# Layer norm from pairwise sums on VectorE and ScalarE, right Strassen factors in a two-engine pipeline, and deferred lower halves in one stage only

## The chip, the core and the metric

The kernel runs on one core of one Trainium2 chip. The metric is the time of one execution in device microseconds (us). TensorE (PE) multiplies, VectorE (DVE) and ScalarE (ACT) do the elementwise work and empty PSUM, GpSimd (POOL) does elementwise work from SBUF to SBUF and issues some DMAs, and SyncE (SP) issues most DMAs. Each engine executes its own instructions in the order in which the program wrote them, and waits for another engine where an operand or a buffer asks for it.

## What is computed

One inference step of a decoder of four layers, 512 prompt positions and 8 sample positions (520 columns in all), model width 1024. Each layer has a token mixer (sparse attention, gated MLP, gated recurrence, sparse attention) and a feed-forward part, and each of the two is followed by a residual sum and a layer norm:

```python
def layer_norm(x, g, b):
    mu = jnp.mean(x, axis=-1, keepdims=True)
    var = jnp.mean(jnp.square(x - mu), axis=-1, keepdims=True)
    return (x - mu) * lax.rsqrt(var + LN_EPS) * g + b

def swiglu_ffn(x, w_in, w_out):
    gate, up = jnp.split(x @ w_in, 2, axis=-1)
    return (jax.nn.silu(gate) * up) @ w_out

for layer in range(4):
    x = layer_norm(ALPHA * x + mixer(x), ...)
    x = layer_norm(ALPHA * x + swiglu_ffn(x, ...), ...)
```

The gated MLP of layer 1 has one more layer norm, on its `v`. So there are nine norms over 520 columns.

## The kernel before

Data lies transposed: the 1024 features are eight blocks of 128 partitions, the 520 columns lie along the free axis, and are worked on in two halves, columns 0 to 255 (the first half) and 256 to 519 (the second half).

**Split products.** Every matrix product runs as three fp32r products: each weight and each activation is split into an upper half (a cast on ACT, L145 for weights, L291 for activations) and a lower half (the source minus the upper half, on DVE, L147 and L292), and `mm` (L330 to L332) multiplies upper by upper, lower by upper and upper by lower. `Weights.need` runs the list of weight splits 5 steps ahead of the one that is used; a step is 4 blocks of k, that is 12 matmuls. `Weights.split` writes the cast at once, but with `lag` on it keeps the lower half back until the next split is written (`flush`). `lag` is on during the whole feed-forward part.

**Ticks.** `mm` calls `tick` after every second k, that is after 6 matmuls. A tick advances every spawned generator by its rate. Layer norm, the right factors and `bounds` are such generators, so their instructions are written between the matmuls of whatever comes next.

**Layer norm** (`ln`, L345). The last product of a half writes the sums over the eight blocks (L442, L444: POOL, the last one DVE). After `WM` = 3 ticks a matmul with a matrix of 1/1024 (L359) gives the mean. Then for four pairs of blocks DVE subtracts it (L366) and ACT squares (L367); DVE reduces each four squared blocks to one row by a strided reduction (L375, two of them); two matmuls (L380) add the two rows over the partitions; ACT and DVE form the reciprocal root (L421 to L434); DVE multiplies by it (L388); ACT writes the upper half with gain and bias (L393); POOL writes the normalised x in place with gain and bias (L397); DVE forms the lower half from x and the upper half (L353), so it waits for POOL. In the last norm's second half `direct` leaves the reductions out and multiplies all eight squared blocks by the matrix.

The out projection goes through the first half of all blocks before the second half, and the next phase begins with first halves only. So the norm of the first half runs beside the out projection's second half, and the norm of the second half beside the first six weight units of the next phase: six times 8 k-blocks of 3 matmuls, 24 ticks.

**Feed-forward.** The 22 hidden blocks are worked on in chunks of 8, 7 and 7. The first 3 blocks of chunk 0 are plain products, whose first halves come first; the others are pairs by Strassen's scheme in Winograd's form, 7 products each (`gated`), in an order that `products` makes. The right factors T1 to T4 are differences of blocks of x, made once (`right`), spawned at the first second-half product at one step per tick: DVE (T3: POOL, L507) writes a difference into an `fsum` tile, ACT casts it, DVE subtracts, and then comes the next. The products of a pair add up in three PSUM banks, by `bank = "xyxzyxx"[q]`; ACT copies bank x out after products 0, 2 and 5 (L577). In the last pair products 5 and 6 are neighbours, both in bank x.

`bounds` prepares constants of layer 2 during the feed-forward part of layer 1, from its 40th tick on: an activation table, one exponential, and some DVE instructions of 32 elements.

## Time and profile before

| what | value |
| --- | --- |
| median of 3 runs | 2996.29 us (2993.99 to 2998.5) |
| the profiled execution | 2996.22 us |
| its span, first to last instruction | 2994.5 us |
| PE busy | 2777.2 us, 93% |
| DVE busy | 2005.7 us, 67% |
| ACT busy | 1555.9 us, 52% |
| POOL busy | 835.3 us, 28% |
| chain of waits that ended last | PE 68%, DVE 16%, ACT 8% |
| granted PE clock, mean | 0.977 |

The profiled execution lies at the median of the runs, and 1.7 us lie outside its span. The engines' shares are averages over stages with different limits. The question for every stage is what PE waits for there.

### The profile page before, as it was taken

How to read it: one execution, taken by the hardware profiler on the slowest of the kernel's cores; microseconds unless marked ns; L12 is line 12 of the kernel's file. 1: busy time of each engine (PE TensorE's matmuls, PEld its weight loads, DVE VectorE, ACT ScalarE, POOL GpSimd, SP SyncE). 2: the span in 40 equal slices, each digit the busy share in tenths (PEclk: the TensorE clock that was granted, in tenths of full speed). 3: DMA queues.
4: the chain of work that ended last, by engine and by line, in shares of the span. 5: the costliest groups of instructions: out<-in, count | busy, mean ns of one | idle time of the engine just before them, and what ended most of it. 6: DMA issues, size and time to landing. Idle time of an engine off the chain costs nothing.

```text
span 2994.5 us, 56333 instructions
## 1 busy us (share of the span) xinstructions
PE 2777.2 (93%) x21818; PEld 2647.2 (88%) x21818; DVE 2005.7 (67%) x4221; ACT 1555.9 (52%) x3474; POOL 835.3 (28%) x787
## 2 busy tenths in 40 slices
PE   7999888999989899998999989999899998899997
PEld 7888568999989899998999989999898875799997
DVE  4788656565756765677677677566768877574665
ACT  4666535454545453554455545345456665453553
POOL 0222134332330432333100033233312222342342
PEclk9999999999999999999999999999999999999998
DMA  4222533555423245562222235556222244345551
GB/s 177 65 64 70 178 127 95 139 156 145 140 78 97 56 130 138 138 173 86 69 83 84 70 104 136 139 140 171 84 89 64 64 135 144 110 120 137 149 158 45
DMA packets 167678, 340.39 MB, mean 114 GB/s; under 512 B 15474, under 2 KB 78450, under 8 KB 167410
## 3 DMA queue, kind: packets, MB, share of 16 engines
q1 hardware_dynamic: 147840, 281.79, 29.6%
q0 software_dynamic: 12096, 44.05, 8.5%
q10 hardware_dynamic: 7474, 10.95, 1.0%
q8 instruction: 172, 2.82, 0.4%
q14 instruction: 96, 0.79, 0.1%
HBM read 323.46 MB, written 13.27 MB: 112 GB/s over the span
## 4 chain that ended last, share of the span: by engine, by line
PE 68%; DVE 16%; ACT 8%; issue 3%; POOL 2%; DMA 2%; SPq 0%; ACTq 0%; POOLq 0%; DVEq 0%
PE ps L330 10%; PE ps L332 10%; PE ps L331 10%; PE ps L530 9%; PE ps L531 8%; PE ps L532 8%; POOL x L397 2%; DVE row L375 2%; ACT g L1164 1%; PE ps L1034 1%; DVE g L1162 1%; PE ps L1211 1%; PE ps L855 1%; PE ps L1160 1%; PE ps L1195 1%
## 5 line engine op out<-in xcount | busy, mean ns | idle before, releaser
L330 PE MATMUL ps<-g 128*128 128x256 f32 (+1 forms) x3744 | 1096.5, 293 | 21.5 <-ACT g L145 13.9
L331 PE MATMUL ps<-g 128*128 128x256 f32 (+1 forms) x3744 | 1070.3, 286 | 29.9 <-DVE g L147 27.2
L332 PE MATMUL ps<-g 128*128 128x256 f32 (+1 forms) x3744 | 1071.2, 286 | 3.4 <-DVE g L292 1.8
L331 PEld LDWEIGHTS ps<-g 128*128 128x128 f32 x3744 | 720.0, 192 | 38.2 <-DVE g L147 29.6
L330 PEld LDWEIGHTS ps<-g 128*128 128x128 f32 x3744 | 720.7, 192 | 34.9 <-ACT g L145 14.1
L332 PEld LDWEIGHTS ps<-g 128*128 128x128 f32 x3744 | 717.8, 192 | 4.6 <-DVE g L292 2.6
L147 DVE TENSOR_TENSOR g<-g 128x512 fp32r<-128x512 f32 x708 | 580.0, 838 | 126.0 <-ACT g L145 125.2
L530 PE MATMUL ps<-g 128*128 128x260 f32 x2128 | 603.6, 284 | 17.5 <-ACT frow L577 17.5
L531 PE MATMUL ps<-g 128*128 128x260 f32 x2128 | 602.1, 283 | 0.0
L532 PE MATMUL ps<-g 128*128 128x260 f32 x2128 | 601.9, 283 | 0.0
L145 ACT CAST g<-g 128x512 fp32r<-128x512 f32 (+1 forms) x788 | 462.0, 607 | 144.8 <-PE ps L332 78.6
L530 PEld LDWEIGHTS ps<-g 128*128 128x128 f32 x2128 | 401.9, 189 | 20.8 <-ACT frow L577 20.8
L532 PEld LDWEIGHTS ps<-g 128*128 128x128 f32 x2128 | 402.1, 189 | 0.0
L531 PEld LDWEIGHTS ps<-g 128*128 128x128 f32 x2128 | 402.1, 189 | 0.0
L577 ACT ACTIVATE frow<-ps 128x260 f32<-128x260 f32 x304 | 117.9, 388 | 247.3 <-PE ps L532 247.3
L1164 ACT ACTIVATE g<-g,nst 128x128 f32<-128x128 f32 (+3 forms) x256 | 143.1, 559 | 123.0 <-DVE nst L1162 120.8
L147 DVE TENSOR_TENSOR g<-fsum,g 128x512 fp32r<-128x512 f32 x228 | 165.1, 724 | 38.3 <-ACT g L145 38.3
L147 POOL TENSOR_TENSOR g<-g 128x512 fp32r<-128x512 f32 x80 | 105.6, 1326 | 249.6 <-ACT g L145 239.1
L1176 POOL TENSOR_SCALAR g<-g,nst 128x128 f32<-128x128 f32 (+3 forms) x64 | 75.9, 1186 | 345.2 <-DVE nst L1169 237.5
L586 POOL TENSOR_TENSOR frow<-frow 128x260 f32<-128x260 f32 x64 | 47.8, 747 | 428.7 <-ACT frow L577 428.7
L180 POOL TENSOR_TENSOR fsum<-g 128x512 f32<-128x512 f32 x76 | 120.9, 1591 | 130.8 <-DMA g<-ffn_in 110.8
L145 ACT CAST g<-fsum 128x512 fp32r<-128x512 f32 x228 | 133.9, 616 | 41.3 <-PE ps L332 41.3
(270 smaller groups left out, 4047.7 us busy)
## 6 DMA issues: line engine op xcount, KB each, us to landing
g<-ffn_in SPq DMA_DIRECT2D x176, 512.0 KB, 4.5
g<-ffn_in POOLq DMA_DIRECT2D x76, 512.0 KB, 5.9
g<-ffn_out SPq DMA_DIRECT2D x64, 448.0 KB, 3.7
g<-nsa_in SPq DMA_DIRECT2D x42, 512.0 KB, 4.3
fsum<-ffn_in SPq DMA_DIRECT2D x76, 256.0 KB, 3.6
cm<-cache_cmp SPq DMA_DIRECT2D x64, 256.0 KB, 3.9
g<-cache_slc SPq DMA_DIRECT2D x128, 128.0 KB, 2.8
g<-cache_win SPq DMA_DIRECT2D x32, 512.0 KB, 4.4
```

What stands on the lines that cost most here:

```text
L145: self.nc.scalar.copy(h, src)
L147: self.subs.append(lambda: (eng or self.nc.vector).tensor_sub(l, src, h.bitcast(FT)))
L180: nc.gpsimd.tensor_add(t[x], t[p], t[q])
L330: nc.tensor.matmul(p[:, :n], H[:, s], a, start=k == 0, stop=False)
L331: nc.tensor.matmul(p[:, :n], L[:, s], a, start=False, stop=False)
L332: nc.tensor.matmul(p[:, :n], H[:, s], b, start=False, stop=k == nk - 1)
L530: nc.tensor.matmul(p, H[:, s], a, start=start and k == 0, stop=False, skip_group_check=True)
L531: nc.tensor.matmul(p, L[:, s], a, start=False, stop=False, skip_group_check=True)
L532: nc.tensor.matmul(p, H[:, s], b, start=False, stop=k == 3, skip_group_check=True)
L577: nc.scalar.activation(s[q], p, AF.Copy, scale=-1.0 if q in (1, 5) else 1.0)
L1164: defer(lambda P=P, i=i: (self.table(LN_EXP), nc.scalar.activation(P, P, AF.Exp, bias=st[:, i:i + 1], scale=-1.0, accum_out=st[:, 4 + i:5 ...
L1176: eng.tensor_scalar(P, P, st[:, 4 + i:5 + i], None, op0=OP.mult)
```

## The change

In `ln`, the reduction is replaced by three additions of 512 or 528 elements, and the matmuls take the two blocks that are left (`direct` is gone, the last norm goes the same way). The squares are written in one tick. `WV` = 2 more ticks lie ahead of the variance matmul. The multiplication by the reciprocal root also applies the gain, one block at a time (two instructions for a pair instead of one). ACT adds the bias when it writes the upper half, DVE forms the lower half from x, the bias and the upper half, and ACT adds the bias to x in place one tick later. POOL is left with one addition for each pair in the norms that write no halves (the gated MLP's and the last).

```diff
-            if j % 2:
-                yield
-        for j in range(2):
-            if direct:
-                q += [sq[j][:, i] for i in range(4)]
-            else:
-                q.append(self.row()[:, :n])
-                nc.vector.tensor_reduce(q[-1], sq[j].rearrange("p b t -> p t b"), op=OP.add, axis=AX.X)
-            yield
+            if j == 3:
+                yield
+        for s in sq:
+            nc.vector.tensor_add(s[:, :2], s[:, :2], s[:, 2:])
+        yield
+        nc.vector.tensor_add(sq[0][:, :2], sq[0][:, :2], sq[1][:, :2])
...
-            nc.vector.tensor_mul(xs, xs, y[:, None, :].to_broadcast([128, 2, n]))
...
+                nc.vector.scalar_tensor_tensor(xs[:, k], xs[:, k], self.gn[:, li, 2 * j + k:2 * j + k + 1], y,
+                                               op0=OP.mult, op1=OP.mult)
             if X is not None:
...
+                for k in (0, 1):
+                    nc.scalar.activation(h[:, k], xs[:, k], AF.Identity, bias=bs[k])
+
+                def low(xs=xs, h=h, l=l, bs=bs):
+                    for k in (0, 1):
+                        nc.vector.scalar_tensor_tensor(l[:, k], xs[:, k], bs[k], h[:, k].bitcast(FT),
+                                                       op0=OP.add, op1=OP.subtract)
+                    after.append(lambda: [nc.scalar.activation(xs[:, k], xs[:, k], AF.Identity, bias=bs[k])
+                                          for k in (0, 1)])
```

On DVE, at the start of the feed-forward part of layer 0, from the second half's sum of blocks to its last lower half (`g<-g 128x512` is a weight's lower half, L147 before and L150 now; L353 before and L398 now is the lower half of x). Before:

```order
L444 TENSOR_TENSOR row<-row,x 128x264
L147 TENSOR_TENSOR g<-g 128x512 x4
L366 TENSOR_TENSOR x<-x,ps 128x2x264 x4
L147 TENSOR_TENSOR g<-g 128x512
L375 TENSOR_REDUCE row<-g 128x264 x2
L624 TENSOR_TENSOR row<-row,ps 128x256
```

and now:

```order
L456 TENSOR_TENSOR row<-row,x 128x264
L150 TENSOR_TENSOR g<-g 128x512 x5
L368 TENSOR_TENSOR x<-x,ps 128x2x264 x4
L373 TENSOR_TENSOR g<-g 128x528 x2
L150 TENSOR_TENSOR g<-g 128x512
L375 TENSOR_TENSOR g<-g 128x528
L643 TENSOR_TENSOR row<-row,ps 128x256
```

Two reductions became three additions, and one more weight's lower half stands ahead of the subtraction, because it is no longer put off.

In `right`, the four factors are made on DVE and ACT alone, in a pipeline over ten steps: the step writes the lower half of the factor before last, the difference for this one, and the cast of the last one. The differences lie in four tiles of the common pool of 39 (`g`) instead of the `fsum` tiles, and the generator runs at 0.6 steps per tick.

```diff
-        for j in range(2):
...
+        for i in range(len(todo) + 2):
+            if i >= 2:
+                n, j = todo[i - 2]
+                v.tensor_sub(part(B[n][1], j), part(t[n], j), part(B[n][0], j).bitcast(FT))
...
+            if 1 <= i <= len(todo):
+                n, j = todo[i - 1]
+                nc.scalar.copy(part(B[n][0], j), part(t[n], j))
+            yield
```

On DVE, the first factors in the feed-forward part of layer 0 (L503, L505 and L509 before and L522, L524 and L527 now are the differences; L292 before and L517 now their lower halves). Before:

```order
L503 TENSOR_TENSOR fsum<-x 128x520
L292 TENSOR_TENSOR g<-fsum,g 128x520
L505 SCALAR_TENSOR_TENSOR fsum<-fsum,x 128x520
L292 TENSOR_TENSOR g<-fsum,g 128x520 x2
L509 SCALAR_TENSOR_TENSOR fsum<-fsum,x 128x520
```

and now:

```order
L522 TENSOR_TENSOR g<-x 128x520 x2
L643 TENSOR_TENSOR row<-row,ps 128x264
L295 TENSOR_TENSOR g<-row,g 128x264
L517 TENSOR_TENSOR g<-g 128x520
L527 SCALAR_TENSOR_TENSOR g<-g,x 128x520
L517 TENSOR_TENSOR g<-g 128x520
L527 SCALAR_TENSOR_TENSOR g<-g,x 128x520
```

A lower half now stands two differences behind its own, and the evacuation of a plain product (L643, L295) comes in between.

In `gated`, the last pair's products 4 and 5 change places, so that product 4 (bank y) stands between the two of bank x. `lag` is switched on for `gated` alone.

```diff
+    k = o.index((n - 1, 4))
+    o[k], o[k + 1] = o[k + 1], o[k]
...
-            self.W.lag, self.W.rawn = True, 4
+            self.W.rawn = 4
...
+            self.W.lag = True
             self.gated(pairs, X, B, hid, m)
+            self.W.flush()
+            self.W.lag = False
```

On DVE, at the last pair of chunk 0 in layer 0 (L580, L583, L590 before and L600, L603, L610 now read products 3, 4 and 6 from PSUM; L586 before and L606 now adds product 5, which ACT has copied out, to product 1). Before:

```order
L580 TENSOR_TENSOR frow<-frow,ps 128x260
L147 TENSOR_TENSOR g<-g 128x512
L583 TENSOR_TENSOR frow<-frow,ps 128x260
L147 TENSOR_TENSOR g<-g 128x512 x2
L586 TENSOR_TENSOR frow<-frow 128x260
L590 SCALAR_TENSOR_TENSOR frow<-ps,frow 128x260
```

and now:

```order
L600 TENSOR_TENSOR frow<-frow,ps 128x260
L150 TENSOR_TENSOR g<-g 128x512 x2
L606 TENSOR_TENSOR frow<-frow 128x260
L603 TENSOR_TENSOR frow<-frow,ps 128x260
L150 TENSOR_TENSOR g<-g 128x512
L610 SCALAR_TENSOR_TENSOR frow<-ps,frow 128x260
```

The sum with product 5 stands ahead of product 4's now.

`bounds` waits 150 ticks instead of 40, which puts it into the first out projection of layer 1's feed-forward part.

## Rows read from the trace of the kernel before

**Rows 1.** By stretch: us, PE, PEld, DVE, ACT, POOL busy (x), PEclk, DMA.

```profile
436.00:520.00 84.00, 72.49 (x554) 70.36 (x553) 59.95 (x90) 39.88 (x75) 33.36 (x34) 0.96 0.31 83
815.00:875.00 60.00, 49.13 (x370) 46.65 (x369) 41.09 (x57) 29.99 (x52) 23.93 (x29) 0.94 0.23 79
890.00:920.00 30.00, 23.94 (x152) 21.88 (x151) 22.28 (x31) 17.32 (x30) 4.41 (x6) 0.83 0.00 1
995.00:1080.00 85.00, 70.57 (x516) 68.51 (x515) 59.57 (x99) 43.48 (x78) 30.19 (x31) 0.92 0.29 74
1375.00:1420.00 45.00, 36.06 (x253) 33.92 (x252) 31.72 (x46) 21.06 (x37) 17.88 (x24) 0.89 0.22 71
1750.00:1830.00 80.00, 68.51 (x534) 66.41 (x533) 58.67 (x89) 40.27 (x76) 30.96 (x33) 0.98 0.32 82
2125.00:2185.00 60.00, 48.19 (x336) 45.14 (x335) 40.62 (x63) 28.21 (x51) 20.23 (x25) 0.89 0.18 59
2575.00:2660.00 85.00, 73.51 (x563) 71.46 (x562) 60.71 (x92) 41.76 (x80) 32.21 (x34) 0.96 0.34 90
2950.00:2978.00 28.00, 23.51 (x170) 22.07 (x168) 15.84 (x26) 7.75 (x13) 8.38 (x11) 0.94 0.11 39
520.00:815.00 295.00, 293.39 (x2449) 292.77 (x2448) 188.48 (x316) 148.78 (x324) 98.15 (x88) 1.00 0.56 150
```

**Rows 2.** PE's waits, whole span: us in total, times, longest.

```profile
PE ps L380 <- DVE row L375: 51.8, 34, 6.3
PE ps L331 <- DVE g L147: 27.2, 10, 7.3
PE ps L530 <- ACT frow L577: 17.5, 16, 4.9
```

**Rows 3.** Timeline of DVE, layer 0's feed-forward start: start us, us.

```profile
468.01 2.54 DVE L366 TENSOR_TENSOR x<-x,ps 128x528 f32<-128x528 f32 x4
...
471.07 3.81 DVE L375 TENSOR_REDUCE row<-g 128x264 f32<-128x1056 f32 x2
```

**Rows 4.** Timeline of PE, the same place; idle time before it in brackets.

```profile
473.07 0.71 PE L380 MATMUL ps<-row,ones 128*128 128x264 f32 x2 [1.57 <-DVE row L375]
```

**Rows 5.** DVE's waits, whole span.

```profile
DVE g L353 <- POOL x L397: 45.4, 53, 1.3
```

**Rows 6.** Timeline of DVE, further on in the same norm.

```profile
485.06 1.80 DVE L353 TENSOR_TENSOR g<-x,g 128x528 fp32r<-128x528 f32 x1 [0.39 <-POOL x L397]
```

**Rows 7.** Timeline of PE, just after that.

```profile
490.06 0.39 PE L331 MATMUL ps<-g 128*128 128x256 f32 x1 [4.25 <-DVE g L147]
```

**Rows 8.** Timeline of DVE, start of layer 1's mixer, second half's norm.

```profile
840.42 0.43 DVE L444 TENSOR_TENSOR row<-row,x 128x264 f32<-128x264 f32 x1 [1.07 <-POOL row L444]
840.77 3.39 DVE L147 TENSOR_TENSOR g<-g 128x512 fp32r<-128x512 f32 x4
...
847.84 0.69 DVE L147 TENSOR_TENSOR g<-g 128x512 fp32r<-128x512 f32 x1 [1.22 <-ACT g L145]
848.45 3.79 DVE L375 TENSOR_REDUCE row<-g 128x264 f32<-128x1056 f32 x2
```

**Rows 9.** Timeline of PE, the same place.

```profile
850.44 1.25 PE L380 MATMUL ps<-row,ones 128*128 128x264 f32 x2 [5.29 <-DVE row L375]
```

**Rows 10.** Timeline of DVE in layer 2's mixer: a three-operand instruction with a per-partition factor.

```profile
1471.65 0.88 DVE L923 SCALAR_TENSOR_TENSOR row<-g,hgain,row 128x256 f32<-128x256 f32 x2
```

**Rows 11.** Lines L393 and L670 on ACT: ns min/median/max, first and last start.

```profile
L393 ACT ACTIVATE g<-x,lngb,lngn x112: 586/594/611, 449.7 to 2624.5; 128x256 fp32r<-128x256 f32 x56, 128x264 fp32r<-128x264 f32 x56
...
L670 ACT ACTIVATE g<-ps,gbin x16: 463/474/483, 839.5 to 896.8; 128x256 f32<-128x256 f32 x8, 128x264 f32<-128x264 f32 x8
```

**Rows 12.** Timeline of DVE, the right factors of layer 0.

```profile
498.04 0.70 DVE L292 TENSOR_TENSOR g<-fsum,g 128x520 fp32r<-128x520 f32 x1 [0.69 <-ACT g L291]
```

**Rows 13.** Timeline of PE: the first pair, then the last pair of chunk 0.

```profile
515.55 0.39 PE L530 MATMUL ps<-g 128*128 128x260 f32 x1 [2.03 <-ACT frow L577]
...
562.33 0.39 PE L530 MATMUL ps<-g 128*128 128x260 f32 x1 [0.54 <-ACT frow L577]
```

More of the change, by code (lines that the diff above doesn't have):

```diff
@@ L343, in order, with ln @@
         return o + [(i, 0) for i in range(n - last, n)] + [(i, 1) for i in range(n - last, n)]
-    def ln(self, cols, li, sums, pair, X=None, out=None, direct=False):
+    def ln(self, cols, li, sums, pair, X=None, out=None):
         nc = self.nc
-        late = []
+        late, after = [], []
         def rest():
-            l, x, h = late.pop(0)
-            nc.vector.tensor_sub(l, x, h.bitcast(FT))
+            late.pop(0)()
         c0, c1 = cols
@@ L360, in ln @@
         yield
-        q, sq = [], []
+        sq = []
         for j in range(4):
@@ L387, in ln @@
             xs = pair(j, c0, c1)
-            nc.vector.tensor_mul(xs, xs, y[:, None, :].to_broadcast([128, 2, n]))
-            hl = X.pair(j) if X is not None else None
+            bs = [self.gb[:, li, 1, 2 * j + k:2 * j + k + 1] for k in (0, 1)]
             for k in (0, 1):
-                g, b = (t[:, li, 2 * j + k:2 * j + k + 1] for t in (self.gn, self.gb[:, :, 1]))
-                if X is not None:
-                    nc.scalar.activation(hl[0][:, k, c0:c1], xs[:, k], AF.Identity, scale=g, bias=b)
-                if X is None and k == 0:
-                    nc.scalar.activation(xs[:, k], xs[:, k], AF.Identity, scale=g, bias=b)
-                else:
-                    nc.gpsimd.tensor_scalar(xs[:, k], xs[:, k], g, b, op0=OP.mult, op1=OP.add)
-            if X is not None:
-                late.append((hl[1][:, :, c0:c1], xs, hl[0][:, :, c0:c1]))
-            elif out is not None:
-                out(j, c0, c1, xs)
+                nc.vector.scalar_tensor_tensor(xs[:, k], xs[:, k], self.gn[:, li, 2 * j + k:2 * j + k + 1], y,
+                                               op0=OP.mult, op1=OP.mult)
+            if X is not None:
+                h, l = (t[:, :, c0:c1] for t in X.pair(j))
+                for k in (0, 1):
[6 more added lines that the diff above has]
+                                          for k in (0, 1)])
+                late.append(low)
+            else:
+                nc.scalar.activation(xs[:, 0], xs[:, 0], AF.Identity, bias=bs[0])
+                nc.gpsimd.tensor_scalar(xs[:, 1], xs[:, 1], bs[1], None, op0=OP.add)
+                if out is not None:
+                    out(j, c0, c1, xs)
+            if after:
+                after.pop(0)()
             if len(late) > 1:
@@ L404, in ln @@
             yield
-        while late:
-            rest()
+        while late or after:
+            if after:
+                after.pop(0)()
+            if late:
+                rest()
             yield
@@ L468, in out_proj @@
                 if m == 7:
-                    X.pend[c0] = self.spawn(self.ln((c0, c1), li, sums[h], self.xpair, None if final else X, out,
-                                                    final and h == 1))
+                    X.pend[c0] = self.spawn(self.ln((c0, c1), li, sums[h], self.xpair, None if final else X, out))
         if li is not None:
@@ L737, in bounds @@
         t = ht[:, 2]
-        yield from wait(40)
+        yield from wait(150)
         nc.vector.tensor_scalar(gain[:, 1:2], gain[:, 0:1], -0.5, None, op0=OP.mult)
```

47 lines of the change are left out of this document (25 added, 22 removed).

## The prediction

> **What bounds the kernel now.** First the table of times: PE is busy for 93% of the span, so little can be had from it but its idle time and its clock. Then the windows by stretch [rows 1]: the reader should compare the last line, a stretch inside a feed-forward part, with the other nine. There 2449 matmuls take 295.00 us at a granted clock of 1.00, or 0.1205 us for one, and DVE has 188.48 us of work. The nine other stretches, each around one or two norms, are slower. Their own time less their count times 0.1205 is 17.3, 15.4, 11.7, 22.8, 14.5, 15.7, 19.5, 17.2 and 7.5 us, 141.6 us in all. Of that, the granted clock (2.4 GHz where the line says 1.00, 1.2 GHz in parts of the rest) accounts for the sum of time times one less PEclk, 37.1 us; the rest is waiting. Next PE's waits [rows 2]: 51.8 us for the reductions, 27.2 us for weights' lower halves though the splits run five steps ahead, and 17.5 us for ACT's copies of a bank. Last the timelines at these places [rows 3 to 9, 12, 13], to see what DVE does while PE waits.
>
> The time I sum against is that of the profiled execution, 2996.22 us: span 2994.5 and 1.7 outside it. The median, 2996.29, is the same number for this purpose.
>
> **Part by part: the variance.** Two reductions take 3.81 us [rows 3]. The three additions have no row. Nearest is the subtraction of as many elements, 2.54/4 = 0.635 us [rows 3]; it reads one operand from PSUM, and 0.70 us is the price of 520 elements from SBUF alone [rows 12]. So they take 1.9 to 2.1 us; I take 2.0 with the last square's wait inside. Before, the first row's matmul could run while the second row was being reduced, up to 0.71 us [rows 4]; now both come at the end. The gain for one half is 3.81 - 2.0 - 0.71 = 1.1, and I take 1.0. Two more ticks stand ahead of the variance matmul, but the squares save one and the additions another, so it stands where it stood: nothing. Nine first halves wait here: **9 us**.
>
> The Trainium skill ("VectorE: DVE Perf Modes", section "The perf-mode tier table (the rule you actually need)") gives a reduction one element per cycle and no faster mode, and an fp32 operation on two tensors the same. By its 0.96 GHz a reduction of 1056 elements would take an estimated 1.10 us, two of them 2.2, and three additions of 528 take 1.65: the change would bring 0.55 us where the rows give 1.8, some 21 us less over 17 halves, and a time of 2940. The trace disagrees, with 1.9 us for one reduction [rows 3], so the measurement decides.
>
> **Second halves at a feed-forward start** (four). Here the norm sits ahead of six weight units, 24 ticks of 6 matmuls, 17.4 us, while DVE also splits weights. At the variance one more weight half comes in ahead of the additions, since it is no longer put off, at 0.69 us [rows 8]: 0.4 of gain is left. Further on PE stands for 4.25 us [rows 7], because the weight half that it wants is behind the norm on DVE. That queue is long because DVE waits for POOL to write x, 45.4 us over 14 halves [rows 5], 3.2 each, and one subtraction beside POOL takes 1.80 us [rows 6] against 0.70 [rows 12]. Both go, as POOL is out of the chain. In their place DVE has 16 short operations for 4 multiplications and 4 subtractions: at 0.88/2 = 0.44 us [rows 10] they take 7.0 us for 4 x 0.635 + 4 x 0.70 = 5.3, so 1.7 more, about what the additions save. Lag is off here now, so DVE stands for a weight's own cast now and then, 1.22 us at a time where it is off today [rows 8]. I leave 1.2 of the 4.25. That is 3.4 for each: **13.6 us**.
>
> The same page, section "The TRN2 errata — SBUF-src ops pay a fixed extra latency per instruction", speaks against halving these operations: 58 cycles for every instruction. An estimate from that is 0.06 us for each of eight more, 0.5 us for a half; the rows' 0.44 twice against 0.635 and 0.70 gives 1.7, so here the trace is harder on the change than the page.
>
> **Second halves at the start of a mixer after the feed-forward part** (three). PE stands for 5.29 us [rows 9]. What DVE goes through before the reductions is a wait of 1.07 for POOL, which is still writing the first half's x when the block sums come; four weight halves, 3.39 instead of 4 x 0.69 because POOL works beside them; and one more that waits 1.22 for its cast [rows 8]. With POOL free the 1.07 go. Without lag three weight halves stand there and not four, 2.0 us: 1.4 less. Of the 1.22 I take 0.7, since the squares ahead of that cast on ACT are written a tick earlier. The additions give 1.0, as above. That is 4.2 for each: **12.6 us**. The gated MLP's v has a second half of its own, where I take the additions and half a microsecond of POOL's, **1.5 us**.
>
> **Right factors.** Of the 17.5 us for bank copies [rows 2], twelve are the last pair's 0.54 [rows 13], 6.5 us; the other four, 11.0 us, stand at the first pair, where PE reaches it before the factors are done (2.03 us in layer 0 [rows 13]; 4.9, the longest, is the place where `bounds` runs beside it). Each step now writes the lower half of an earlier factor, so the 0.69 us for the cast [rows 12] goes eight times, 5.5 us, against two more differences on DVE at 0.70. This closes the 2.03. `bounds` moves into an out projection, where PE's work is weights and evacuations alone; I cost it at nothing, and if that cover fails, at up to 4.9. The four become zero: **11 us**. Four tiles more of the 39 are held meanwhile; loads there use 0.31 of the DMA engines [rows 1], so I expect no hold.
>
> **The pair of products.** Twelve times 0.54 [rows 13] and some 0.1 around it: **7.7 us**. The new neighbour works in bank y, whose DVE read stands two products away.
>
> **Lag.** It is off for the plain products and out projections. DVE has 188.48 us of work in 295.00 [rows 1], so a cast's wait there is slack: nothing, with 120 us as the bound above (below, third rival).
>
> **The clock.** The low stretches are those of the longest waits: 0.89 and 0.83 where PE stands 5 to 7 us, 0.96 to 0.98 where it stands at most some 4 [rows 1]. With what is left of the waits under 3 us I expect 0.98 everywhere: of 37.1 us lost, 0.02 x 557 = 11.1 remain, and 26 come back. Only the busy part of it counts, 466 of 557 us: **22 us**.
>
> Sum: 9 + 13.6 + 12.6 + 1.5 + 11 + 7.7 + 22 = 77.4, or 2996.2 - 77.4 = **2919 us**.
>
> **Rivals.** *ACT becomes the bound at the second halves.* It now writes bias into x as well as the upper half: 16 instructions at 0.474 [rows 11] for eight at 0.594, 2.8 us more for a half, between the casts on which DVE's weight halves now depend at once. For it: lag is gone just there. Against: ACT is half idle in the nine stretches [rows 1]. If PE waits for all of it in seven second halves, 20 us go, and 12 of the clock's 22 with them: 2951 us.
>
> *The stalls close altogether.* The 1.2 us that I leave at each feed-forward start, the 1.1 at each mixer's second half and as much again at the first halves go too, DVE having lost POOL's waits: 4.8 + 3.3 + 9.9, and the clock's last 11.1: 29 us more, 2890 us.
>
> *Weights late without lag, slower.* 240 weight steps, 192 of the out projections and 48 of the plain products, now stand at DVE's head until their cast is done, and evacuations queue behind, so that PE gets no bank. From 77/240 = 0.32 us each the gain is gone; at 0.5 it is 120 us, 3039 in all. For it: DVE does wait for L145, up to 1.22 us at a time [rows 8]. Against: the mixers run without lag, and splits are five steps ahead of use.
>
> *Nothing is won*, because PE is then held by the weights' casts at the same places, moving each wait to the next instruction: within 0.2% of 2996, which is 6 us and about what a measurement can tell from no change. The waits are of three separate kinds, so all would have to be replaced.
>
> **How the numbers follow.** Forecast 0.53, ACT the bound 0.22, stalls closed 0.20, slower 0.03, nothing 0.02. My forecast's own bounds: additions 1.9 to 2.1 over 17 halves (2 us either way), residual stalls at double (9) or none (9), the clock at 0.97 or 0.99 (5), `bounds` 4.9, in all about 2900 to 2938. With the first rival's 2951 and the second's 2890, each a little beyond its point, the range is 2884 to 2953. Faster by over 0.2%: 0.95; within: 0.02; slower: 0.03.
>
> **What would show it.** PE's waits: those for the variance's DVE line at about half of 51.8 us, those for weight halves under 12, those for bank copies near zero, with no 0.54 at last pairs. DVE's waits for POOL at the lower half gone. PEclk 0.97 or more in all nine stretches. Out projections at 0.1205 us for a matmul; if they are slower, the third rival holds. I am wrong if POOL's absence leaves ACT's casts as the new releaser of PE and DVE at second halves (the first rival), if short operations cost over 0.5 us each, or if the clock stays low though the waits are short.

## The result

The changed kernel takes 2957.53 us (median of 4 runs, 2954.06 to 2960.58) against 2996.53: a ratio of 0.987, 95% interval 0.9853 to 0.9887. It is 39 us faster where 77 were forecast, and 4.5 us above the upper end of the range. Half of the gain is missing.

PE's waits in the changed kernel (us in total, times, longest), those that answer to [rows 2]:

```profile
PE ps L379 <- DVE g L375: 48.7, 18, 6.7
PE ps L550 <- ACT frow L597: 16.0, 4, 4.2
...
PE ps L334 <- DVE g L150: 9.9, 4, 7.4
```

The wait for the variance is nearly what it was, 48.7 us for 51.8. Laid apart by place, the nine first halves wait 9.2 us in all where they waited 17.4, and the nine second halves 39.5 where they waited 35.9. The waits for weight halves fell from 27.2 to 9.9, and 7.4 of that is one wait 20 us into the program, which no edit touches. The wait for ACT's copies, which was to go to zero, holds 16.0 us in only four waits: the twelve of 0.54 at the last pairs are gone, and the four first pairs wait longer than before. The stretches that answer to [rows 1], between the same places of the program to within 3 us:

```profile
436.00:518.00 82.00, 71.42 (x548) 70.12 (x549) 60.57 (x108) 43.72 (x89) 18.50 (x18) 0.96 0.32 84
811.00:866.00 55.00, 49.85 (x388) 48.95 (x387) 39.90 (x76) 34.77 (x68) 12.31 (x14) 0.97 0.25 87
880.00:907.00 27.00, 20.34 (x139) 19.36 (x138) 18.27 (x35) 16.25 (x28) 5.81 (x5) 0.87 0.00 1
983.00:1062.00 79.00, 68.95 (x520) 67.62 (x519) 58.04 (x107) 45.45 (x91) 12.29 (x13) 0.94 0.30 79
1354.00:1393.00 39.00, 33.81 (x246) 32.77 (x245) 29.66 (x59) 22.72 (x44) 10.91 (x14) 0.91 0.28 95
1723.00:1801.00 78.00, 69.34 (x524) 67.87 (x523) 58.86 (x108) 44.37 (x90) 12.36 (x13) 0.93 0.31 80
2094.00:2151.00 57.00, 45.95 (x338) 43.95 (x338) 38.85 (x81) 33.14 (x66) 7.12 (x9) 0.91 0.18 62
2544.00:2626.00 82.00, 72.64 (x566) 71.41 (x565) 60.96 (x113) 46.58 (x95) 15.11 (x16) 0.96 0.34 93
2912.00:2938.00 26.00, 23.44 (x183) 22.47 (x181) 14.09 (x30) 6.62 (x11) 10.15 (x11) 1.00 0.12 41
```

The granted clock is 0.87 to 0.97 in eight of the nine stretches, where 0.97 or more was forecast for all. By the prediction's own sum (time times one less PEclk) 30.6 us are lost, after 37.1. Times the busy share that the prediction used, 466 of 557, that is about 5 of the 22 us forecast for the clock.

At the first feed-forward start, timelines of DVE, ACT and PE (start, us, engine, line; idle time before it in brackets):

```profile
488.41 0.88 DVE L398 SCALAR_TENSOR_TENSOR g<-x,lngb,g 128x264 fp32r<-128x264 f32 x2
490.40 0.69 DVE L150 TENSOR_TENSOR g<-g 128x512 fp32r<-128x512 f32 x1 [1.11 <-ACT g L148]
...
494.25 0.42 DVE L643 TENSOR_TENSOR row<-row,ps 128x256 f32<-128x256 f32 x1 [2.34 <-ACT row L642]
```

```profile
489.76 0.61 ACT L148 CAST g<-g 128x512 fp32r<-128x512 f32 x1
...
491.60 0.92 ACT L400 ACTIVATE x<-x,lngb 128x264 f32<-128x264 f32 x2 [0.40 <-DVE g L398]
492.54 1.28 ACT L426 ACT_TABLE_LOAD   x1
493.83 0.39 ACT L642 ACTIVATE row<-ps 128x256 f32<-128x256 f32 x1
```

```profile
513.94 0.58 PE L550 MATMUL ps<-g 128*128 128x260 f32 x1 [4.16 <-ACT frow L597]
```

GpSimd is out of DVE's chain at the lower halves of x, as expected. But DVE stands for ACT's cast, ACT for DVE's lower half, and DVE again for the evacuation that ACT writes after its bias additions and a table load. PE meets the delay 20 us later, at the first pair.

To compare whole programs I number the weight matmuls: every kernel here runs the same 17,616 (three of 3744 and three of 2128) in one order, but for the exchanged products, so the start of a given one can be set against the start of the same one in the kernel before. The differences between two such numbers, grouped by place (us against before, each from one trace):

| kernel | four feed-forward starts | three mixer starts | pairs and out projections |
| --- | --- | --- | --- |
| the changed kernel | -14.3 | -17.3 | -7.1 |
| norm alone | -6.7 | -15.7 | +0.2 |
| right factors alone | -13.1 | +1.3 | +0.7 |
| exchanged products alone | +0.9 | -0.7 | -7.6 |
| lag in pairs alone | +19.8 | -0.2 | 0.0 |
| changed, lag as before | -26.9 | -17.5 | -7.0 |
| the best kernel below | -28.3 | -19.2 | -6.9 |

One start is the stretch that 436 to 527, 980 to 1085, 1715 to 1830 or 2540 to 2660 us are in the kernel before; a mixer start 815 to 880, 1340 to 1425 or 2090 to 2185. What no column holds is up to 5 us either way. In the changed kernel the gated MLP and the last norm are part of it (1.4 and 2.7 us gained); the rest lies in stages that no edit touches, and its cause is not shown.

### The profile page after: what moved, and what is told of

Read it like the earlier page. It is cut to its first block, busy times and chain, and to the rows that moved or that the text cites. A ratio compares the mean times of both kernels' runs of the same rounds, so it can differ in the third digit from the quotient of the medians.

```text
span 2955.7 us, 56427 instructions
## 1 busy us (share of the span) xinstructions
PE 2759.2 (93%) x21806; PEld 2638.9 (89%) x21806; DVE 2006.7 (68%) x4377; ACT 1589.9 (54%) x3586; POOL 729.5 (25%) x667
## 4 chain that ended last, share of the span: by engine, by line
PE 65%; DVE 11%; ACT 7%; issue 2%; DMA 1%; SPq 0%; POOL 0%; ACTq 0%; POOLq 0%; DVEq 0%
PE ps L333 10%; PE ps L335 10%; PE ps L334 10%; PE ps L550 9%; PE ps L552 9%; PE ps L551 9%; PE ps L877 1%; ACT g L369 1%; DVE g L150 1%; ACT g L148 1%; PE ps L1233 1%; PE ps L1217 1%; PE ps L1056 1%; PE ps L1182 1%; ACT g L1186 1%
## 5 line engine op out<-in xcount | busy, mean ns | idle before, releaser
L333 PE MATMUL ps<-g 128*128 128x256 f32 (+1 forms) x3744 | 1093.0, 292 | 22.1 <-ACT g L148 14.5
L334 PEld LDWEIGHTS ps<-g 128*128 128x128 f32 x3744 | 716.0, 191 | 19.3 <-DVE g L150 10.8
L150 DVE TENSOR_TENSOR g<-g 128x512 fp32r<-128x512 f32 x708 | 585.6, 845 | 155.5 <-ACT g L148 152.6
L150 DVE TENSOR_TENSOR g<-fsum,g 128x512 fp32r<-128x512 f32 x228 | 163.5, 717 | 35.3 <-ACT g L148 35.3
L606 POOL TENSOR_TENSOR frow<-frow 128x260 f32<-128x260 f32 x64 | 48.0, 751 | 546.9 <-ACT frow L597 546.9
L150 POOL TENSOR_TENSOR g<-g 128x512 fp32r<-128x512 f32 x80 | 105.6, 1326 | 276.6 <-ACT g L148 266.1
```

What stands on the lines that cost most here:

```text
L150: self.subs.append(lambda: (eng or self.nc.vector).tensor_sub(l, src, h.bitcast(FT)))
L333: nc.tensor.matmul(p[:, :n], H[:, s], a, start=k == 0, stop=False)
L334: nc.tensor.matmul(p[:, :n], L[:, s], a, start=False, stop=False)
```

## The experiments

Times are medians; all were run beside the kernel before (2994.5 to 2996.9 us).

| kernel | us | ratio to before, 95% interval |
| --- | --- | --- |
| b_ln | 2974.24 | 0.9925 (0.9912 to 0.9937) |
| b_right | 2987.37 | 0.997 (0.9961 to 0.9978) |
| b_swap | 2983.89 | 0.9964 (0.9952 to 0.9977) |
| b_lag | 3011.36 | 1.0051 (1.0034 to 1.0068) |
| a_early2 | 2958.61 | 0.9877 (0.9862 to 0.9891) |
| a_nolow | 2936.34 | 0.980 (0.9784 to 0.9816) |
| a_nobias | 2938.56 | 0.9806 (0.979 to 0.9823) |
| a_evac | 2953.63 | 0.986 (0.9842 to 0.9879) |
| a_add1 | 2957.21 | 0.987 (0.9852 to 0.9888) |
| a_latebias | 2955.01 | 0.9862 (0.9845 to 0.9878) |
| a_evac_latebias | 2942.01 | 0.982 (0.9804 to 0.9836) |
| a_poolbias | 2967.67 | 0.9909 (0.9893 to 0.9926) |
| a_lag | 2942.45 | 0.9827 (0.981 to 0.9843) |
| a_lag_evac | 2940.48 | 0.9809 (0.979 to 0.9827) |
| a_lag_evac_late | 2934.29 | 0.9793 (0.9777 to 0.981) |
| a_lag_evac_late_add1 | 2937.07 | 0.9808 (0.9792 to 0.9824) |

### Parts of the change alone

**The norm** (`ln` as in the change, `WV` = 2, the rest as before).

```diff
-WM, WV = 3, 0
+WM, WV = 3, 2
...
-                nc.vector.tensor_reduce(q[-1], sq[j].rearrange("p b t -> p t b"), op=OP.add, axis=AX.X)
+            nc.vector.tensor_add(s[:, :2], s[:, :2], s[:, 2:])
```

> The kernel before with the layer norm alone (additions for reductions, gain on DVE, bias on ACT, two ticks more ahead of the variance). By the terms of the prediction for the norms, 9 + 13.6 + 12.6 + 1.5, it gains 37 us without any clock. Theory 'passed on': the norms give that, but the four first pairs take back 3 to 4 us each, so PE's wait for bank copies rises from 17.5 us to 28 or more and the time falls by 20 to 27 us. Rival 'ACT the bound' (the bias additions hold up the casts of weights): the waits for weights' lower halves stay above 20 us of their 27.2 and the time falls by less than 15 us.

PE's waits:

```profile
PE ps L376 <- DVE g L372: 46.6, 18, 6.6
PE ps L538 <- ACT frow L585: 30.9, 16, 8.7
```

It is 22.7 us faster, inside the first theory's span. At the mixers it gains 15.7 us, where 12.6 and three first halves of 1.0 were forecast; 10.4 of it is PE's idle time (a stretch less PE's busy time in it), the rest PE's busy time. At the feed-forward starts it gains 6.7 for a forecast of 17.6, and the difference is in the rows: the wait for bank copies is 30.9 us, less twelve of 0.54 it is 24.4, where the kernel before had 11.0. Those 13.4 us and the 6.7 make 20.1. By this sum the norm gave at least what was expected, and the first pair took two thirds of it back.

**The right factors** (`right` as in the change, at 0.6 steps a tick).

```diff
-                    right = self.spawn(self.right(X, B), 1)
+                    right = self.spawn(self.right(X, B), 0.6)
```

> The kernel before with the new pipeline of right factors alone (its rate of 0.6 steps per tick too). In the changed kernel PE waits four times for ACT's copy at the first pair, 16.0 us in all, where it waited 11.0 before and where the prediction had zero. Theory 'passed on': the pipeline is shorter, but PE now comes to the first pair some 4 us earlier, because its waits in the norm are shorter, and finds the factors undone. Then the pipeline alone must close most of the 11.0 here: PE's wait for the bank copies falls from 17.5 us to 6.5 (the last pairs) plus at most 3, and the time falls by 8 to 12 us. Rival 'no shorter': the sixteen DVE instructions of 0.61 us that follow each other make a chain of 9.8 us from a later start, as long as the old one; then the wait stays above 14 us and the time moves by less than 4 us.

```profile
PE ps L539 <- ACT frow L586: 10.1, 14, 3.4
```

Of the 10.1 us twelve of 0.54 are the last pairs; 3.6 are left of 11.0, a little more than the 3 I had allowed. Three of the four first pairs no longer wait; 3.43 us are one wait in layer 1, where `bounds` still runs beside the factors in this kernel. It is 9.6 us faster in all, and 13.1 us in the four stretches: some 7 of PE's idle time and 6 of its busy time, at a granted clock of 0.97 to 0.98 where it was 0.93 to 0.98. In the old surroundings the term "right factors" was right for the waits.

No run has the move of `bounds` alone, but the first pairs show its price. With `bounds` at its old place, layer 1's first pair waits some 3 us longer than those of the other layers: 4.9 us for 2.0 in the kernel before, 8.7 for 4.3 to 5.8 in b_ln, 10.0 for 7.0 in b_lag. In the changed kernel it waits 4.2 us, and the others 3.5 to 4.2.

**The exchanged products.**

```diff
+    k = o.index((n - 1, 4))
+    o[k], o[k + 1] = o[k + 1], o[k]
```

> The kernel before with products 4 and 5 of the last pairs exchanged, nothing else. Prediction's term: 12 x 0.64 = 7.7 us. The two traces, laid over each other by the number of the matmul, show 0.77 to 0.9 at each such place, 9 to 10 us. The 0.54 waits at the last pairs go; time 7 to 10 us lower, nothing else moves. Rival: the sum with product 5 and the evacuation of product 4 meet on DVE, which keeps a part; then under 4 us.

```profile
PE ps L533 <- ACT frow L580: 11.0, 4, 4.9
```

The twelve short waits are gone and the four others stay. In the stretches of the pairs it gains 7.6 us, the term's 7.7; by the ratio it is 10.8 us faster, and the rest lies outside the pairs, in stages that the edit does not touch.

**The lag.**

```diff
-            self.W.lag, self.W.rawn = True, 4
+            self.W.rawn = 4
...
+            self.W.lag = True
             self.gated(pairs, X, B, hid, m)
+            self.W.flush()
+            self.W.lag = False
```

> The kernel before with the lower halves of weights put off in the pairs alone, nothing else. Undoing this one edit in the changed kernel brought 15 us, where the prediction had the edit at nothing. Theory 'the lag costs by itself': at the second halves' starts DVE then stands for casts whatever norm runs there, so the kernel before also becomes slower, by 6 to 15 us, all of it in the four feed-forward starts, while out projections keep their pace. Rival 'only with the new norm': the cost is there because the new norm has ACT write the bias between the casts; then the kernel before, whose GpSimd does that, moves by less than 4 us.

It costs by itself: 15 us by the ratio, 19.8 in the four feed-forward starts, and nothing in the out projections. PE's waits:

```profile
PE ps L380 <- DVE row L375: 57.5, 34, 6.2
PE ps L530 <- ACT frow L577: 37.5, 16, 10.0
...
PE ps L331 <- DVE g L147: 7.9, 2, 7.3
```

PE no longer stands for weight halves (7.9 us for 27.2), but the first pairs wait 20.0 us longer (37.5 for 17.5) and the variance 5.7. DVE in layer 0, from the sum of blocks on:

```profile
466.27 3.10 DVE L147 TENSOR_TENSOR g<-g 128x512 fp32r<-128x512 f32 x5
...
473.04 0.69 DVE L147 TENSOR_TENSOR g<-g 128x512 fp32r<-128x512 f32 x1 [1.22 <-ACT g L145]
473.65 3.78 DVE L375 TENSOR_REDUCE row<-g 128x264 f32<-128x1056 f32 x2
...
481.51 0.69 DVE L147 TENSOR_TENSOR g<-g 128x512 fp32r<-128x512 f32 x1 [2.07 <-ACT g L145]
482.12 0.43 DVE L430 SCALAR_TENSOR_TENSOR row<-ps,row 128x264 f32<-128x264 f32 x1
```

and ACT:

```profile
470.02 2.48 ACT L367 ACTIVATE g<-x 128x528 f32<-128x528 f32 x4 [10.25 <-DVE x L366]
472.41 0.60 ACT L145 CAST g<-g 128x512 fp32r<-128x512 f32 x1
...
478.73 1.28 ACT L414 ACT_TABLE_LOAD   x1
480.03 0.48 ACT L421 ACTIVATE row<-ps,eps 128x264 f32<-128x264 f32 x1
...
480.87 0.60 ACT L145 CAST g<-g 128x512 fp32r<-128x512 f32 x1
```

A weight half that is no longer put off stands in DVE's queue where its cast has just been written. The cast is on ACT behind the norm's own squares, or behind the table load and the root; DVE waits 1.22 and 2.07 us for it, with the norm's next instruction queued behind (L375, L430). Over the whole run, DVE's waits for casts, in the kernel before and then in this one:

```profile
DVE g L147 <- ACT g L145: 163.5, 197, 13.0
```

```profile
DVE g L147 <- ACT g L145: 182.3, 205, 13.0
```

Over the run that is 18.8 us more. Of these waits 3.3, 5.4, 4.6 and 4.6 us lie in the four feed-forward starts, 15 in number, where the kernel before has 2.7 us in four. So it is not 240 steps at a small price each, but some fifteen in these four places, at about 1.2 us; the two above stand in the norm's chain. The 15.2 us more that DVE waits there come back on PE as 14.0 us of idle time and 5.4 of busy time, at a granted clock of 0.89 to 0.94 where it was 0.93 to 0.98. So the price is not waits alone, and the match of 18.8 with 19.8 is not one of like with like.

### What the first pair waits for

First theory: the factors begin too late. Begun right behind the norm:

```diff
+        while any(g.gi_frame is not None for g in norms):
+            yield
...
-                if h == 1 and right is None:
-                    right = self.spawn(self.right(X, B), 0.6)
+            if right is None:
+                right = self.spawn(self.right(X, B, list(X.pend.values())), 0.6)
```

> The changed kernel with its right factors begun as soon as the second half's norm has written its last instruction (up to six ticks earlier in the program), at the same rate; nothing else is changed. Theory 'passed on': the factors' start is what is late; begun some 4 us earlier, they are done when PE comes, its wait for bank copies falls from 16.0 us to under 4, and the time falls by 10 to 16 us against the changed kernel (2957 to about 2944). Rival 'DVE is full': the sixteen instructions push back the weights' lower halves and the plain products' evacuations, PE's waits for these grow by about what the first pair gives back, and the time stays within 4 us.

```profile
PE ps L552 <- ACT frow L599: 15.8, 4, 4.0
```

The theory fell: the wait is 15.8 us for 16.0, the time 1 us higher. The factors are early now, and the plain products' evacuations, which stand ahead of ACT's copy in its queue, are late instead: in layer 0 the last cast of a factor ends at 504.5 us (511.6 in the changed kernel), and that of an evacuation at 508.6. Next theory: DVE is full. From 473 to 513 us the kernel before and the changed one read (DVE is the third busy column):

```profile
473.00:513.00 40.00, 33.99 (x259) 33.10 (x260) 29.11 (x45) 20.64 (x40) 17.41 (x16) 0.96 0.17 41
```

```profile
473.00:513.00 40.00, 34.16 (x262) 33.48 (x262) 32.89 (x56) 24.14 (x50) 7.16 (x6) 0.96 0.26 60
```

In just this stretch the change puts 3.8 us more on DVE and 3.5 more on ACT; GpSimd's 17.41 us became 7.16. To test it I took work from either engine. From DVE, the lower halves of the factors:

```diff
-            if i >= 2:
-                n, j = todo[i - 2]
-                v.tensor_sub(part(B[n][1], j), part(t[n], j), part(B[n][0], j).bitcast(FT))
```

> The changed kernel without the lower halves of the right factors: the eight subtractions of 128x520 in each layer are left out (the third matmul of each product reads the upper half in their place), so the output is not the reference's. From the norm's variance to the first pair of layer 0 the changed kernel's DVE is busy for 32.6 of 39.6 us, while PE's 262 matmuls need 31.6 at full pace; and starting the factors earlier left PE's wait for the bank copies at 15.8 us. Theory 'DVE is full from the variance to the first pair': every microsecond of DVE work taken out there comes back. Eight times 0.61 = 4.9 us a layer: PE's wait for bank copies falls from 16.0 us to under 4, the time falls by 12 to 18 us against the changed kernel (2957). Rival 'it is the order': ACT's copy waits for the plain products' evacuations, which come after the casts whatever DVE does; the wait stays above 10 us and the time falls by less than 6.

and from ACT, the bias on x:

```diff
-                    after.append(lambda: [nc.scalar.activation(xs[:, k], xs[:, k], AF.Identity, bias=bs[k])
-                                          for k in (0, 1)])
```

> The changed kernel without ACT's addition of the bias to x in place (8 instructions of about 0.40 us for each half of the seven norms that write halves; the residual and the right factors then lack the bias, the output is not the reference's). The prediction's rival 'ACT becomes the bound at the second halves': 22 us of ACT work in the seven second halves go, and the time falls by 10 to 20 us. Theory 'DVE is full': ACT is busy for 23.8 of 39.6 us in the same stretch, DVE alone sets it; the time falls by less than 4 us.

Waits for bank copies in the first, then in the second:

```profile
PE ps L547 <- ACT frow L594: 2.1, 4, 0.7
```

```profile
PE ps L548 <- ACT frow L595: 7.8, 4, 2.0
```

The first is 21 us faster than the changed kernel, the second 19. Both leave work out and serve as tests only; the first also frees four tiles and takes away a matmul's wait for the lower half, so not all of its 21 us need be DVE's time. "DVE is full" has no room for the second result, since nothing was taken from DVE; "ACT is the bound" has none for the first. Both engines lie on one chain: each runs in the order of the program and hands every piece to the other, so what is taken from either shortens it. GpSimd is no way out:

```diff
-                    after.append(lambda: [nc.scalar.activation(xs[:, k], xs[:, k], AF.Identity, bias=bs[k])
+                    after.append(lambda: [nc.gpsimd.tensor_scalar(xs[:, k], xs[:, k], bs[k], None, op0=OP.add)
```

> The changed kernel with the bias added to x by GpSimd in place of ACT, the same instructions in the same place. It takes the 3.3 us a half from ACT as leaving them out did (18 us in all), but GpSimd then works beside DVE. In the changed kernel DVE's lower halves of x take 0.49 us alone and 1.53 and 2.21 beside GpSimd. Theory 'one chain, and GpSimd stretches DVE's part': DVE loses about half of what ACT wins, the time lies 0 to 10 us under the changed kernel's 2957. Rival 'ACT is full': most of the 18 us are there, 2944 or less. Rival 'contention decides': slower than 2960.

```profile
PE ps L550 <- ACT frow L597: 26.5, 4, 6.6
```

It is 10 us slower than the changed kernel, the third of the three answers: 26.5 us at the first pairs, where leaving the same work out had 7.8. GpSimd takes 1.05 us for an addition that ACT makes in 0.50 (medians), but no instruction waits for one directly. DVE is what slows down: in the four feed-forward starts it is busy for 309.8 us, and for 294.3 in the changed kernel.

### Reordering without taking work out

Three edits of the changed kernel: the evacuation of plain products taken apart over two ticks (a_evac), the third addition directly behind the first two (a_add1), and the bias on x behind all lower halves (a_latebias).

```diff
-                nc.vector.tensor_mul(g, g, pu[:, :w])
-                hid.put(j, c0, c1, g)
+                    nc.vector.tensor_mul(g, g, pu[:, :w])
+                    nc.scalar.copy(h, g)
+                    yield
+                    nc.vector.tensor_sub(l, g, h.bitcast(FT))
+                self.spawn(evac())
```

> The changed kernel with the plain products' evacuation taken apart: DVE's multiplication and ACT's cast are written one tick after ACT's silu, and DVE's subtraction one tick after that, so that DVE does not stand for ACT's silu and cast (about 0.47 us, twice for each of six evacuations in a layer). No work is left out. Theory 'DVE is full': some 3 to 5 us of DVE's idle time between dependent steps goes for each feed-forward start, PE's wait for bank copies falls from 16.0 us to 2 to 8, and the time by 8 to 14 us. Rival 'it is the order': wait and time stay within 4 us.

```diff
-        yield
         nc.vector.tensor_add(sq[0][:, :2], sq[0][:, :2], sq[1][:, :2])
-        yield from wait(WV)
+        yield from wait(WV + 1)
```

> The changed kernel with the third addition written in the same tick as the first two, so that no weight's lower half stands between them; the variance matmul stays at its tick. In the second halves that weight half takes 0.61 us, and 2.20 where GpSimd works beside it. PE's wait for the additions, 48.7 us in 18 waits, falls by 0.6 to 2 us at each of seven second halves, 6 to 9 us. Theory 'DVE is full': what is gained at the four feed-forward starts is found again at the first pair, since the weight half has only changed places, so the time falls by only 2 to 4 us, that of the mixers' starts. Rival: each wait counts by itself, the time falls by 6 to 9 us.

```diff
-            if after:
-                after.pop(0)()
...
+        yield
+        while after:
+            after.pop(0)()
+            yield
```

> The changed kernel with ACT's additions of the bias to x put off until all lower halves of the norm are written, one pair a tick; no work is left out. Leaving those additions out brought 18 us and leaving out eight DVE subtractions 20 us, so neither engine alone is full: from the variance to the first pair DVE and ACT hand work to each other in program order, and a microsecond taken from either comes back. Theory 'one chain through both engines': in the changed kernel four of the additions stand between the last cast and the table load ahead of the first evacuation, where DVE then has nothing for 2.3 us; put off into ACT's own idle time they cost nothing there, PE's wait for bank copies falls from 16.0 us to 8 to 12, and the time falls by 6 to 14 us against the changed kernel (2957). Rival 'ACT is full': its work is the same, later, so the time stays within 4 us.

Alone they bring 4, 0 and 2.5 us by the medians, less than I expected of each, and none is clear of noise: the three intervals overlap that of the changed kernel. a_evac's wait for bank copies falls to 10.6 us, but waits for casts of weights rise from 14.5 to 22.5; a_add1 moves 5.5 us from the variance (43.2) to other waits; a_latebias has 19.6 at the first pairs. Each seems to clear one link, and the next holds. The first and the third together:

> Both reorderings together: the late bias and the evacuation taken apart. Alone the second brought 4 us, PE's wait for bank copies at 10.6 us for 16.0. Theory 'one chain through both engines': the two remove different idle times, so they add up, wait for bank copies under 7 us, 10 to 18 us faster than the changed kernel (2939 to 2947). Rival: what the one frees the other had already freed; no more than 3 us better than the better of the two.

15.5 us faster than the changed kernel by the medians, more than the 6.5 of the two alone, with 10.2 us of bank waits left (I had said under 7). That is hardly less than the 10.6 of a_evac, and the execution that was traced took 2947.48 us, 3.6 less than a_evac's. So where the median's gain lies is not shown. Then the lag of before in the changed kernel:

```diff
-            self.W.rawn = 4
+            self.W.lag, self.W.rawn = True, 4
...
-            self.W.lag = True
             self.gated(pairs, X, B, hid, m)
-            self.W.flush()
-            self.W.lag = False
```

> The changed kernel with the lower halves of weights put off in the whole feed-forward part again, as before. The prediction cost that edit at nothing and gave it a bound of 120 us. Laid over each other by the number of the matmul, the two traces show out projections and pairs unchanged but for 0.8 us at each last pair, so it is cheap there; at the heads of the second halves DVE stands for a cast now, 1.1 to 1.5 us at a time. Theory 'one chain through both engines': with lag on the cast is there already, and the time falls by 2 to 8 us, or stays. Rival: the lag matters where the prediction did not look; the time rises by over 4 us.

15.1 us faster, twice what I expected at most. DVE's waits for casts in the changed kernel, and with the lag of before:

```profile
DVE g L150 <- ACT g L148: 187.9, 213, 10.8
```

```profile
DVE g L150 <- ACT g L148: 170.1, 202, 10.8
```

PE's wait at the first pairs falls from 16.0 us to this:

```profile
PE ps L550 <- ACT frow L597: 2.8, 2, 1.4
```

The combinations:

> The changed kernel with the lag of before and the evacuation taken apart. Alone they brought 15 and 4 us. Theory 'one chain through both engines': with the lag, PE's waits at the first pairs are already at 0 to 1.7 us, so there is little left to give back there; 2 to 6 us better than the lag alone (2936 to 2940). Rival: they add up in full to 19 us or more, or the subtraction put off delays a weight half and the sum is under the lag's 15.

> The changed kernel with the lag of before, the evacuation taken apart and the late bias, candidates for a version better than both. Theory 'one chain through both engines': late bias brought nothing alone (2 us) but 12 on top of the evacuation, because the one removed DVE's wait for the other; here I expect 3 to 8 us more than the lag alone, 2934 to 2939, with the waits left at the variance (second halves, 2 to 7 us each), which none of the three touches. Rival: 'the variance is all that is left': within 3 us of the lag alone.

> The same with the third addition in the tick of the first two. In the changed kernel this moved 5.5 us of PE's wait for the additions (48.7 to 43.2) into other waits and left the time where it was (2957.2 for 2957.5). Theory 'one chain through both engines': it only moves a weight half behind the addition, so again within 3 us of the run without it. Rival: with the later waits gone, the 5 us stay won.

With lag and evacuation 2940.48, at the edge of what I expected, with the late bias too **2934.29 us**, ratio 0.9793 (0.9777 to 0.981). This is the best kernel here, 23 us under the changed one and 62 under the one before. Against the lag alone it is 8 us better by the medians, where the two intervals just touch; the third addition adds nothing. What it still waits for:

```profile
PE ps L379 <- DVE g L375: 47.3, 18, 7.0
PE ps L334 <- DVE g L150: 20.6, 8, 7.4
```

None of this kernel's three additional edits touches the 47.3 us at the variance. The third addition does, 41.0 us in a_lag_evac_late_add1, and the time does not follow.

## Why the prediction was wrong

**Lag: "nothing".** This step failed first. The cover was named, "DVE has 188.48 us of work in 295.00" [rows 1], but that row is of the pairs and the out projections, and there the cover held. The lag was also taken from the plain products, where the same group has DVE at 59.95 of 84 us and a norm in its queue. Rows 8 held the price: a weight half that waits 1.22 us for its cast, in a mixer, where lag was off already. I used it as a residual of 1.2 in the second-half term, once a start, and weighed the rest as 240 equal small costs. It costs 15 us (b_lag), and putting the lag back brings 15 (a_lag).

**The clock: 22 us.** About 5 came (37.1 us lost before, 30.6 now). The waits did not get shorter: at the variance 48.7 us are in 18 waits instead of 34, and the longest is 6.7. With the lag of before (a_lag) the same nine stretches lose some 21 us, in the best kernel some 22: part of the missing clock belongs to the lag. I had reckoned with waits under 3 us everywhere, so this term hung on the others.

**Right factors: 11 us to zero.** The waits were sized right: alone the edit takes 7.4 of the 11.0 us, and the 3.43 left are the place of `bounds`. That b_right gains 13.1 in the stretches is partly luck, since some 6 of it is busy time. In the changed kernel the four waits still came out at 16.0. The step that failed is treating the first pair as a place of its own. It is the end of the chain that begins at the second half's norm; gains of the norm arrive there as an earlier PE and an unchanged last evacuation. Alone, the norm gains 6.7 us at these starts and the factors 13.1; with the lag's cost of 19.8 and 0.9 of the exchange the four parts sum to +0.9, with some 3 of `bounds` to about -2, and together they are -14.3. What such a part is worth depends on what else stands on the chain.

**Variance at second halves.** I had 0.4 to 1.0 us for each. The four feed-forward starts waited 2.7 us each, and wait 2.34, 4.22, 2.81 and 4.68 now. In layer 0 the term held: one wait of 2.34 us, where two of 1.57 [rows 4] and 1.14 were.

```profile
473.79 1.16 PE L379 MATMUL ps<-g,ones 128*128 128x264 f32 x4 [2.34 <-DVE g L375]
```

In the other three an addition met GpSimd's sums of weights. DVE and GpSimd in layer 1's feed-forward start:

```profile
1009.81 2.46 DVE L373 TENSOR_TENSOR g<-g 128x528 f32<-128x528 f32 x2
1012.20 2.20 DVE L150 TENSOR_TENSOR g<-g 128x512 fp32r<-128x512 f32 x1
1014.32 0.69 DVE L375 TENSOR_TENSOR g<-g 128x528 f32<-128x528 f32 x1
```

```profile
1010.45 1.26 POOL L183 TENSOR_TENSOR fsum<-g 128x512 f32<-128x512 f32 x1 [6.90 <-DMA g<-ffn_in]
...
1012.27 1.57 POOL L183 TENSOR_TENSOR fsum<-fsum,g 128x512 f32<-128x512 f32 x1
```

From the first addition to the end of the third, with a weight half between, it is 5.2 us, where the same four take 2.7 by themselves (471.01 to 473.73 in layer 0); the reductions took 3.8 [rows 3]. The bound of 0.70 that I took for an addition from SBUF was of an operation without GpSimd beside it. Over the run six of the 54 additions are longer, 5.3 us in all. The last norm's second half, which had no reductions before (`direct`), waits 4.8 us where it waited 1.5, but its matmuls take 2.1 us for 5.5, so its time is the same. The Trainium skill ("GPSIMD Engine Reference", section "1. Specifications") says that GpSimd's SBUF interfaces are shared with VectorE, with contention for DVE instructions that have two SBUF inputs; the trace agrees, with 2.46 us for two additions that take 1.50 in layer 0, and this is a rule against the change that I did not weigh.

**What held.** The variance at the nine first halves (8.2 us less wait for 9 forecast), the exchanged products (7.6 for 7.7), no wait for GpSimd at the lower halves, `bounds` without a price in its new place (pairs and out projections gain 1.6 us in layer 1, 1.4 to 2.5 in the others), and out projections at their old pace, so the third rival's mechanism was the right one in the wrong place. The norm at the mixers (15.7 for 15.6) is partly luck: 10.4 us are waits, and 5.3 are busy time, which the forecast had under the clock. The weight-half waits (9.9, under 12) met their sign but not for the reason given alone: taking the lag off lowers them to 7.9 by itself (b_lag), and with the lag of before they are 20.0 in a kernel that is 15 us faster (a_lag). A short wait there was in part a wait moved to the first pair. The first rival, ACT's bias additions, took 20 us of waits and 12 of the clock off the gain and forecast 2951. Leaving these additions out brings 19 us in all (a_nobias), and work taken from DVE brings as much, so ACT is half of a chain and not the bound by itself.

Not tried: the weights' pair sums away from GpSimd at the variance, which would tell how much of the 47 us there is its doing. So the account of the second halves is read from traces and not shown by an experiment.

## To carry to other kernels

Where two engines hand work back and forth in program order, neither share of busy time is a cover: follow one item through both queues to the next place where PE must have it, and price every edit on that chain by the end of the chain. An edit that takes away a delay ("written at once instead of one later") costs at the places where the delayed instruction's source is itself queued behind the work that now waits. And take the cover for an edit from the stretch in which the edited instructions stand, not from the stage that is easiest to read.

## What the runs showed of the hardware

DVE operations from two SBUF operands took longer beside GpSimd's sums of weights (L180 before). In the kernel before, 112 of the lower halves of weights (L147) ran for more than half of their time beside such a sum; their median is 1.48 us, and 0.68 for those with no such sum beside them. An operation with one operand in PSUM kept its time: 24 of the 76 below ran wholly beside such a sum (ns, least, median, most).

```profile
L590 DVE SCALAR_TENSOR_TENSOR frow<-ps,frow x76: 428/429/430, 525.9 to 2929.2; 128x260 f32<-128x260 f32 x76
```

The first two additions of a half in the changed kernel did not always keep theirs:

```profile
L373 DVE TENSOR_TENSOR g<-g x36: 682/693/2209, 444.5 to 2940.8; 128x512 f32<-128x512 f32 x18, 128x528 f32<-128x528 f32 x18
```

Whether a reduction would keep its time is not shown: none of the 34 in the kernel before ran beside a sum of weights. Five had another GpSimd operation beside them for some 0.7 us and kept their 1.94 to 2.01 us. But six additions, too, had other GpSimd operations beside them and kept their 0.68 to 0.69.
